# Down projection by blocks: sums one step ahead of the splits, plain tiles in the written order

## The chip, the core and the metric

The kernel runs on one core of one Trainium2 chip. The metric is device time in microseconds (us). Three runs of the kernel before gave 2416.98, 2417.23 and 2417.55 us; the median is 2417.23 us.

## The reference

The program computes two layers. Each layer has three parts, and in each the input is normalised, worked on, normalised again and added to the residual `x`. Parts one and three are feed-forward networks (SwiGLU), part two is a mixer of three branches. The change touches the feed-forward networks alone, of which there are four in a run.

```python
SEQ, D_MODEL, D_FF, DEPTH = 512, 1024, 2816, 2

def swiglu_ffn(h, w_gate, w_up, w_down):
    return (jax.nn.silu(h @ w_gate) * (h @ w_up)) @ w_down

for l in range(DEPTH):
    h = rms_norm(x, norm_pre[l, 0])
    x = x + 0.5 * rms_norm(swiglu_ffn(h, ffn1_w_gate[l], ffn1_w_up[l], ffn1_w_down[l]), norm_post[l, 0])
    ...
```

All of it is float32. The **down projection** is the last product, `hidden @ w_down`: 512 tokens by 2816 hidden values, times 2816 by 1024.

## The kernel before

**Precision.** Every operand of a matmul is split into a high part of type float32r and the rest: `hi = cast(x)` on ACT (ScalarE), `lo = x - hi` on DVE (VectorE). A product then takes three matmuls: high by high, high by low and low by high (`mm_out`, L248). So each operand costs a cast on ACT and a subtraction on DVE before PE (TensorE) can use it, and the subtraction waits for the cast.

**The hidden values** lie transposed, in 22 tiles `hid[f]` of 128 hidden values by 512 tokens. `block_tiles` (L346) makes them, and then the down projection follows.

**The down projection before** is the class `Down` (L466). Hidden tiles 2 to 17 are multiplied by blocks, with seven products in place of eight (the scheme of Strassen and Winograd): the hidden values, the tokens and the output columns are each cut into two halves, and sums and differences of blocks are multiplied. The seven products are named in `ORDER` (L470) after their left block: A11, S3, S2, A12, S1, S4, A22. Each has four **steps** c0 to c3 (`PER` is 4), and a step takes two hidden tiles: 12 matmuls of 512 columns. Tiles 0 and 1 (`MIDDLE`) and 18 to 21 (`LAST`) are multiplied plainly, 24 matmuls a tile: the two `MIDDLE` tiles after the product S1, the four `LAST` ones at the end, in `out_proj` (L253), one token tile after the other.

**What a step needs** stands in `prepare` (L497): load the weights (512 KB a quadrant; SP, the sync engine, issues all loads); where the step has a weight sum, form it on DVE (1024 columns; in products S3, S2, S1 and A22); for S2 also two sums of hidden values on DVE; then the casts `dh` and `whi` on ACT, the subtractions `dl` and `wlo` on DVE; for A12 two more sums of hidden values. In S3 a step loads two quadrants, and its sum frees them at once, since it is kept in the room of `xh`. In the other products the quadrant stays in its buffer until the step's `wlo` is done.

**What sets the order.** `run` (L573) first prepares four steps (`AHEAD`), and then, after the matmuls of step d, prepares step d+4. All that `prepare` issues on ACT and DVE is pinned: it stays in written order on its engine. `classical` (L564) makes the plain tiles: it is written after product S1, it loads, splits and multiplies at that place, and its splits go through `split` (L111), which isn't pinned, so the scheduler may place them among pinned work. `out_proj` does the same for `LAST` with the function `stat` in `ffn` (L707).

**Buffers.** `whi` and `wlo` have five each. `raw`, the loaded weights, has three tiles of two halves each; a load waits until both halves of an older tile are used up. `dh` and `dl` come from the 14 slots "s".

Of the kernel before, what the change touches and what calls it, by code (L numbers as in the profile page):

```python
# [8 lines left out]
F32 = mybir.dt.float32  # L9
F32R = mybir.dt.float32r  # L10
# [31 lines left out]
def kernel(  # L42
# [30 lines left out]
    def slot(name, dt=F32, tag="t"):  # L73
        return tp.tile([P, 512], dt, tag=tag, name=name, bufs=SLOTS[tag])

    def bank(n, tag="pb"):
        return psp.tile([P, 512], F32, tag=tag, name=n, bufs=BANKS[tag])
# [172 lines left out]
        mm(o, sh[:, t], wl, start=False, stop=False, skip_group_check=True)  # L250
        mm(o, sl[:, t], wh, start=False, stop=en, skip_group_check=True)

    def out_proj(w2d, nk, stat, tail, finish, upcoming, early, banks=None):  # L253


        ld = lambda k: load_rows(w2d, k)
        fresh = banks is None
# [208 lines left out]
    class Down:  # L466
# [5 lines left out]
        STEPS = 7 * PER  # L472
        AHEAD = 4
        MIDDLE, LAST = (0, 1), (18, 19, 20, 21)

        def __init__(self, wd, hid):
            self.wd, self.hid = wd, hid
            self.ready = {}
            self.s1 = None
            self.next = 0  # L480

        def pairs(self):

# [10 lines left out]
            else:  # L494
                pinned(nc.vector.tensor_tensor(a[:, H1], a[:, H0], a[:, H1], op=ALU.add))

        def prepare(self, d):  # L497

            if d >= self.STEPS:
                return  # L500
            j, c = divmod(d, self.PER)
            name, quads, _ = self.ORDER[j]
            f0 = self.F0 + 2 * c
            raws = []
            for half, h in quads:
                r0 = (f0 + half * self.NP) * P
                raws.append(load_raw([(lambda r: r.rearrange("p (k c) -> p k c", k=2),
                                       self.wd[r0:r0 + 2 * P, HS[h]].rearrange("(k p) c -> p k c", p=P))]))
            kept = None if j == 0 else self.kept[:, 2 * c:2 * c + 2, :].rearrange("p k c -> p (k c)")
            tt = lambda o, a, b, op: pinned(nc.vector.tensor_tensor(o, a, b, op=op))  # L510
# [12 lines left out]
            a = [self.hid[f0 + q] for q in range(2)]  # L523
            b = [self.hid[f0 + self.NP + q] for q in range(2)]
# [3 lines left out]
            part = {"A11": [x[:, H0] for x in a], "S3": [x[:, H1] for x in a], "S2": [x[:, H0] for x in a],  # L528
                    "A12": [x[:, H0] for x in b], "S4": [x[:, H0] for x in b], "A22": [x[:, H1] for x in b],
                    "S1": None}[name]  # L530
            sh, sl = (slot(x, F32R, "s").rearrange("p (k t) -> p k t", k=2) for x in ("dh", "dl"))
            hi, lo = (wp.tile([P, 1024], F32R, tag=t, name=t) for t in ("whi", "wlo"))
            if part is None:
                pinned(nc.scalar.copy(sh, self.s1[c]))
            else:
                for q in range(2):
                    pinned(nc.scalar.copy(sh[:, q], part[q]))
            pinned(nc.scalar.copy(hi, src))  # L538
            if part is None:
                tt(sl, self.s1[c], sh.bitcast(F32), ALU.subtract)  # L540
            else:
                for q in range(2):
                    tt(sl[:, q], part[q], sh[:, q].bitcast(F32), ALU.subtract)
            tt(lo, src, hi.bitcast(F32), ALU.subtract)
            if name == "A12":
                for q in range(2):
                    tt(b[q][:, H0], b[q][:, H0], a[q][:, H0], ALU.add)
            self.ready[d] = sh, sl, hi, lo

        def ahead(self):  # L550
            self.prepare(self.next)
            self.next += 1

        def product(self, d):
            j, c = divmod(d, self.PER)
            name, _, b = self.ORDER[j]
            sh, sl, hi, lo = self.ready.pop(d)
            for q in range(2):
                w = slice(q * 512, (q + 1) * 512)
                for i in range(2):  # L560
                    mm_out(self.banks[b][i], slice(i * P, (i + 1) * P), sh[:, q], sl[:, q], hi[:, w], lo[:, w],
                           st=(q == 0 and c == 0 and j in (0, 1, 3)))

        def classical(self, f, first):  # L564

            wh, wl = load_rows(self.wd, f)
            sh, sl = slot("sh", F32R, "s"), slot("sl", F32R, "s")
            split(sh, sl, self.hid[f])
            for i, h in ((2, 1), (3, 1), (2, 0), (3, 0), (0, 0), (1, 0), (0, 1), (1, 1)):
                mm_out(self.out[i][h], slice(i * P, (i + 1) * P), sh, sl, wh[:, HS[h]], wl[:, HS[h]],  # L570
                       st=(first and (i, h) in ((2, 1), (3, 1))))

        def run(self):  # L573
            a0, b0, a1, b1, c0, d0 = (bank(n) for n in ("oA", "oB", "oA", "oB", "oC", "oD"))
# [6 lines left out]
            copy = lambda o, i: pinned(nc.scalar.copy(o, i))  # L581
            while self.next < self.AHEAD:
                self.ahead()
            for d in range(self.STEPS):
                j, c = divmod(d, self.PER)
                self.product(d)
                self.ahead()
                if c < self.PER - 1:
                    continue
                if j == 0:  # L590
                    for i in range(2):
                        copy(self.p1[i], self.banks["A"][i])
                if j == 1:
                    for i in range(2):
                        copy(p7[i], self.banks["C"][i])
                if j == 2:
                    self.u2 = [slot("u2") for i in range(2)]
                    for i in range(2):
                        copy(self.u2[i], self.banks["A"][i])
                if j == 4:  # L600
                    self.u4 = [slot("u4") for i in range(2)]
                    for i in range(2):
                        copy(self.u4[i], self.banks["A"][i])
                    for i in range(2):
                        pinned(nc.vector.tensor_tensor(self.u4[i], p7[i], self.u4[i], op=ALU.subtract))
# [21 lines left out]
    def ffn(wg, wu, wd, weights, forms, arrive, finish, upcoming, early, late, begin):  # L627
# [76 lines left out]
        block_tiles(wg, wu, fs, forms, hid, between)  # L704
        late()

        def stat(f):  # L707
            sh, sl = slot("sh", F32R), slot("sl", F32R)
            split(sh, sl, hid[f])
            return sh, sl  # L710

        banks = down.run()
        return out_proj(wd, NF, stat, TAIL, lambda i, b: finish(i, down.results(i, b)), upcoming, early, banks)


    def mixer(l, wv, arrive, finish, upcoming, early):
# [585 lines left out]
```

## Time and profile before

| | us |
|---|---|
| median of three runs | 2417.23 |
| profiled execution | 2419.53 |
| its span, first to last instruction | 2417.8 |
| ACT busy | 1218.4 (50%) |
| POOL busy | 179.0 (7%) |
| time of DMA queue q1, as a share of 16 engines | 35.9% |

The profile comes from one execution. Its span is 1.7 us shorter than that run's time, and that run is 2.3 us longer than the median. For each engine the profile lists busy time; for each instruction its start, its duration, the idle time of the engine ahead of it and, where it can be told, what ended that idle time. The duration of a matmul is the time until its end is modelled; the next one starts earlier, since matmuls are pipelined. The order in which the span runs is: first layer FFN 1, mixer, FFN 2, then the second layer the same way. The four down projections begin near 244, 1081, 1444 and 2280 us.

### The profile page before, as it was taken

How to read it: one execution, taken by the hardware profiler on the slowest of the kernel's cores; microseconds unless marked ns; L12 is line 12 of the kernel's file. 1: busy time of each engine (PE TensorE's matmuls, PEld its weight loads, DVE VectorE, ACT ScalarE, POOL GpSimd, SP SyncE). 2: the span in 40 equal slices, each digit the busy share in tenths (PEclk: the TensorE clock that was granted, in tenths of full speed). 3: DMA queues.
4: the chain of work that ended last, by engine and by line, in shares of the span. 5: the costliest groups of instructions: out<-in, count | busy, mean ns of one | idle time of the engine just before them, and what ended most of it. 6: DMA issues, size and time to landing. Idle time of an engine off the chain costs nothing. (4 is left out here: it accounts for less than half of the span.)

```text
span 2417.8 us, 36165 instructions
## 1 busy us (share of the span) xinstructions
PE 2339.3 (97%) x14072; PEld 2064.9 (85%) x14072; DVE 1855.4 (77%) x2745; ACT 1218.4 (50%) x2372; POOL 179.0 (7%) x287
## 2 busy tenths in 40 slices
PE   8999989999999999998999998999999999999988
PEld 7999767887888899996799996778878888999956
DVE  7888867858965388888688888678599644888885
ACT  5556545644323355565455565466433334555552
POOL 0000001201011100000000000012010211000000
PEclk9999999999999999999999999999999999999999
DMA  5333543231333233345323345341313332333441
GB/s 167 105 105 108 205 141 97 71 92 47 112 87 105 79 87 103 104 134 192 115 83 105 105 131 190 119 115 53 109 49 107 89 105 64 98 106 104 167 161 70
DMA packets 332764, 265.33 MB, mean 110 GB/s; under 512 B 12746, under 2 KB 285164, under 8 KB 332592
## 3 DMA queue, kind: packets, MB, share of 16 engines
q1 hardware_dynamic: 332592, 263.02, 35.9%
q8 instruction: 110, 1.80, 0.3%
q14 instruction: 62, 0.51, 0.1%
HBM read 260.88 MB, written 2.10 MB: 109 GB/s over the span
## 5 line engine op out<-in xcount | busy, mean ns | idle before, releaser
L352 DVE TENSOR_TENSOR wlo<-raw,whi 128x1024 fp32r<-128x1024 f32 (+1 forms) x304 | 331.1, 1089 | 108.8 <-ACT whi L350 108.0
L113 DVE TENSOR_TENSOR wlo<-raw,whi 128x1024 fp32r<-128x1024 f32 (+1 forms) x202 | 252.4, 1257 | 200.5 <-ACT whi L112 193.7
L112 ACT CAST whi<-raw 128x1024 fp32r<-128x1024 f32 (+1 forms) x202 | 210.6, 1045 | 387.2 <-PE gate L66 131.3
L350 ACT CAST whi<-raw 128x512 fp32r<-128x512 f32 x532 | 315.4, 620 | 160.0 <-DVE raw L352 160.0
L352 DVE TENSOR_TENSOR raw<-raw 128x512 f32<-128x512 f32 x304 | 209.2, 688 | 5.8
L66 PE MATMUL A<-xh,whi 128*128 128x256 f32 x608 | 172.5, 284 | 0.0
L66 PE MATMUL A<-xh,wlo 128*128 128x256 f32 x608 | 172.0, 283 | 0.0
L66 PE MATMUL A<-xl,whi 128*128 128x256 f32 x608 | 172.0, 283 | 0.0
L892 DVE SCALAR_TENSOR_TENSOR y<-u,cw,y 128x511 f32<-128x511 f32 (+14 forms) x240 | 166.7, 756 | 0.0
L66 PE MATMUL gate<-xh,whi 128*128 128x512 f32 x384 | 151.3, 394 | 0.0
L66 PE MATMUL gate<-xh,wlo 128*128 128x512 f32 x384 | 149.8, 390 | 1.3 <-DVE wlo L113 1.3
L66 PE MATMUL gate<-xl,whi 128*128 128x512 f32 x384 | 149.6, 390 | 0.0
L200 POOL TENSOR_TENSOR rs<-ms,mhalf 128x1 f32<-128x1 f32 x48 | 28.2, 588 | 1513.1 <-DVE ms L198 1513.1
L510 DVE TENSOR_TENSOR wlo<-raw,whi 128x1024 fp32r<-128x1024 f32 x80 | 97.8, 1222 | 50.1 <-ACT whi L538 50.1
L538 ACT CAST whi<-raw 128x1024 fp32r<-128x1024 f32 x80 | 84.1, 1051 | 93.3 <-PE oA L66 38.1
L66 PE MATMUL oA<-wlo,dh 128*128 128x512 f32 x256 | 103.5, 404 | 18.5 <-DVE wlo L510 18.5
L350 ACT COPY cp<-A 128x256 f32<-128x256 f32 x228 | 84.5, 370 | 70.6 <-PE A L66 69.7
L66 PEld LDWEIGHTS A<-xl,whi 128*128 128x128 f32 x608 | 116.6, 192 | 0.2
L66 PEld LDWEIGHTS A<-xh,whi 128*128 128x128 f32 x608 | 116.5, 192 | 0.2
L66 PEld LDWEIGHTS A<-xh,wlo 128*128 128x128 f32 x608 | 116.6, 192 | 0.0
L66 PE MATMUL oA<-whi,dh 128*128 128x512 f32 x256 | 101.3, 396 | 4.8 <-ACT whi L538 4.8
L66 PE MATMUL oA<-whi,dl 128*128 128x512 f32 x256 | 100.0, 390 | 0.0
(346 smaller groups left out, 7183.8 us busy)
## 6 DMA issues: line engine op xcount, KB each, us to landing
raw<-in_ffn_w_down_dram SPq DMA_DIRECT2D x152, 512.0 KB, 4.6
raw<-in_w_in_dram SPq DMA_DIRECT2D x108, 512.0 KB, 4.7
raw<-in_ffn_w_gate_dram SPq DMA_DIRECT2D x152, 256.0 KB, 3.4
raw<-in_ffn_w_up_dram SPq DMA_DIRECT2D x152, 256.0 KB, 4.6
raw<-in_w_branch_dram SPq DMA_DIRECT2D x24, 512.0 KB, 3.7
raw<-in_w_out_dram SPq DMA_DIRECT2D x16, 512.0 KB, 4.2
raw<-in_ffn_w_gate_dram SPq DMA_DIRECT2D x12, 512.0 KB, 5.1
raw<-in_ffn_w_up_dram SPq DMA_DIRECT2D x12, 512.0 KB, 4.6
```

The costliest lines, as they stand in the source:

```text
L66: tc.keep_in_program_order(nc.tensor.matmul(*a, **k))
L112: nc.scalar.copy(hi, src)
L113: nc.vector.tensor_tensor(lo, src, hi.bitcast(F32), op=ALU.subtract)
L200: nc.gpsimd.tensor_tensor(rs, ms, mhalf[:, 0:1], op=ALU.pow)
L350: copy = lambda o, i: pin(nc.scalar.copy(o, i))
L352: tt = lambda o, a, b, op: pin(nc.vector.tensor_tensor(o, a, b, op=op))
L510: tt = lambda o, a, b, op: pinned(nc.vector.tensor_tensor(o, a, b, op=op))
L538: pinned(nc.scalar.copy(hi, src))
L892: nc.vector.scalar_tensor_tensor(y[:, back:], u[:, :S - back], cw[:, c, j:j + 1], y[:, back:], op0=ALU.mult, op1=ALU.add)
```

## The change

`prepare` is divided in two. `sums(p)` issues the loads of step p and then what it adds up on DVE: the weight sum, and for S2 first the two sums of hidden values and then the weight sum. `parts(p)` issues the casts and the two kinds of subtraction. `ahead` calls `sums(p + 1)` and then `parts(p)`, so on DVE the sums of a step stand in front of the subtractions of the step before it.

The plain tiles become steps as well. `plan` writes one list: five products (A11 to S1), `MIDDLE`, the products S4 and A22, `LAST`. `classical` and `stat` are gone; a plain tile is loaded by `sums`, split by `parts` and multiplied by `product`, four steps behind its preparation. `out_proj` gets the four `LAST` tiles ready-made (`head`). The splits of the plain tiles are thereby pinned, their slots are those of `dh` and `dl`, and the cast and subtraction of S1 and of plain tiles go over 512 columns at once. The matmuls and their order on PE stay as they were, and so does the number of instructions of each kind on ACT and DVE.

```diff
-    def out_proj(w2d, nk, stat, tail, finish, upcoming, early, banks=None):
+    def out_proj(w2d, nk, stat, tail, finish, upcoming, early, head=None):
...
+        else:
+            banks, rest = head
...
-        rest = [(k, ld(k), stat(k)) for k in range(nk - tail, nk)]
+        if fresh:
+            rest = [(k, ld(k), stat(k)) for k in range(nk - tail, nk)]
...
+        def plan(self):
+
+            self.steps = [(j, c) for j in range(5) for c in range(self.PER)]
+            self.steps += [(None, f) for f in self.MIDDLE]
+            self.steps += [(j, c) for j in (5, 6) for c in range(self.PER)]
+            self.end = len(self.steps)
+            self.steps += [(None, f) for f in self.LAST]
...
+        def sums(self, p):
+
+            self.load(p)
+            j, c = self.steps[p]
+            if j is None:
+                return
+            name, raws = self.ORDER[j][0], self.raw[p]
...
             if name == "S2":
+                for q, x in enumerate(self.of(p)):
+                    tt(x, self.s1[c][:, q], x, ALU.add)
                 tt(kept, kept, raws[0], ALU.subtract)
                 src = kept
...
-            if name == "S2":
-                for q in range(2):
-                    tt(a[q][:, H0], self.s1[c][:, q], a[q][:, H0], ALU.add)
...
+        def parts(self, p):
+
+            j, c = self.steps[p]
+            sh, sl = (slot(x, F32R, "s") for x in ("dh", "dl"))
             hi, lo = (wp.tile([P, 1024], F32R, tag=t, name=t) for t in ("whi", "wlo"))
...
+            of, src = self.of(p), self.raw.pop(p)
+            n = 512 // len(of)
+            cut = [slice(q * n, (q + 1) * n) for q in range(len(of))]
+            for q, x in zip(cut, of):
+                pinned(nc.scalar.copy(sh[:, q], x))
             pinned(nc.scalar.copy(hi, src))
...
+            for q, x in zip(cut, of):
+                pinned(nc.vector.tensor_tensor(sl[:, q], x, sh[:, q].bitcast(F32), op=ALU.subtract))
+            pinned(nc.vector.tensor_tensor(lo, src, hi.bitcast(F32), op=ALU.subtract))
...
         def ahead(self):
-            self.prepare(self.next)
+
+            p = self.next
+            if p == 0:
+                self.sums(0)
+            if p + 1 < len(self.steps):
+                self.sums(p + 1)
+            if p < len(self.steps):
+                self.parts(p)
             self.next += 1
...
-        def classical(self, f, first):
-
-            wh, wl = load_rows(self.wd, f)
-            sh, sl = slot("sh", F32R, "s"), slot("sl", F32R, "s")
-            split(sh, sl, self.hid[f])
...
             while self.next < self.AHEAD:
                 self.ahead()
-            for d in range(self.STEPS):
-                j, c = divmod(d, self.PER)
-                self.product(d)
+            for p in range(self.end):
+                j, c = self.steps[p]
+                self.product(p)
                 self.ahead()
...
-                    for f in self.MIDDLE:
-                        self.classical(f, f == self.MIDDLE[0])
-            return self.out
+            while self.next < len(self.steps):
+                self.ahead()
+            rest = []
+            for p in range(self.end, len(self.steps)):
+                sh, sl, hi, lo = self.ready[p]
+                rest.append((self.steps[p][1], (hi, lo), (sh, sl)))
+            return self.out, rest
```

Three places show it. The first is DVE where product S2 begins, in the first down projection. `xh` is the kept weight sum, `hid<-S` the two sums of hidden values, `dl` and `wlo` the low parts. Before, from the low part of step S3 c3 through step S2 c1:

```order
L510 TENSOR_TENSOR wlo<-xh,whi 128x1024
L510 TENSOR_TENSOR xh<-xh,raw 128x1024
L510 TENSOR_TENSOR hid<-S_648,hid 128x256 x2
L510 TENSOR_TENSOR dl<-hid,dh 128x256 x2
L510 TENSOR_TENSOR wlo<-xh,whi 128x1024
L510 TENSOR_TENSOR xh<-xh,raw 128x1024
L510 TENSOR_TENSOR hid<-S_649,hid 128x256 x2
L510 TENSOR_TENSOR dl<-hid,dh 128x256 x2
L510 TENSOR_TENSOR wlo<-xh,whi 128x1024
```

Now, from the sums of step S2 c0 to the low parts of the same step:

```order
L540 TENSOR_TENSOR hid<-S_648,hid 128x256 x2
L540 TENSOR_TENSOR xh<-xh,raw 128x1024
L569 TENSOR_TENSOR dl<-hid,dh 128x256 x2
L570 TENSOR_TENSOR wlo<-xh,whi 128x1024
L540 TENSOR_TENSOR hid<-S_649,hid 128x256 x2
L540 TENSOR_TENSOR xh<-xh,raw 128x1024
L569 TENSOR_TENSOR dl<-hid,dh 128x256 x2
L570 TENSOR_TENSOR wlo<-xh,whi 128x1024
```

The sums of a step have moved past the low parts of the step before: between a sum and the low part made from it there now stand the other step's `dl` and `wlo` and the next step's sums.

The second place is DVE where the down projection begins. Before, from the low parts of step A11 c3 (`wlo<-raw`) to the second weight difference of S3:

```order
L510 TENSOR_TENSOR dl<-hid,dh 128x256 x2
L510 TENSOR_TENSOR wlo<-raw,whi 128x1024
L510 TENSOR_TENSOR xh<-raw 128x1024
L510 TENSOR_TENSOR dl<-hid,dh 128x256 x2
L510 TENSOR_TENSOR wlo<-xh,whi 128x1024
L510 TENSOR_TENSOR xh<-raw 128x1024
```

Now, from the first weight difference of S3 (step c0) to the third:

```order
L540 TENSOR_TENSOR xh<-raw 128x1024
L569 TENSOR_TENSOR dl<-hid,dh 128x256 x2
L570 TENSOR_TENSOR wlo<-raw,whi 128x1024
L540 TENSOR_TENSOR xh<-raw 128x1024
L569 TENSOR_TENSOR dl<-hid,dh 128x256 x2
L570 TENSOR_TENSOR wlo<-xh,whi 128x1024
L540 TENSOR_TENSOR xh<-raw 128x1024
```

Each weight difference, and with it the need for its loaded quadrants, has moved ahead by one pair of low parts.

The third place is ACT around the `MIDDLE` tiles. `u` is a copy of a PSUM bank that frees it for the plain tiles; `sh` (before) and `dh<-hid 128x512` (now) are the high parts of plain hidden tiles. Before, from the last step of S4 that is prepared ahead:

```order
L537 CAST dh<-hid 128x256 x2
L538 CAST whi<-raw 128x1024
L581 COPY u_3559<-oA 128x512
L581 COPY u_3560<-oA 128x512
L112 CAST whi<-raw 128x1024
L112 CAST sh<-hid 128x512 x4
L537 CAST dh<-hid 128x256 x2
L112 CAST sh<-hid 128x512
L112 CAST whi<-raw 128x1024
L538 CAST whi<-raw 128x1024
```

Now, from the first `MIDDLE` tile through the copies:

```order
L566 CAST dh<-hid 128x512
L567 CAST whi<-raw 128x1024
L566 CAST dh<-hid 128x512
L567 CAST whi<-raw 128x1024
L566 CAST dh<-hid 128x256 x2
L567 CAST whi<-raw 128x1024
L566 CAST dh<-hid 128x256 x2
L567 CAST whi<-raw 128x1024
L613 COPY u_3557<-oA 128x512
L613 COPY u_3558<-oA 128x512
```

Both `MIDDLE` tiles have moved ahead of all four steps of S4, of which two now stand ahead of the copies, and the cast of the second tile's weights has moved up to that of the first.

More of the change, by code (lines that the diff above doesn't have):

```diff
@@ L251, in mm_out @@
         mm(o, sl[:, t], wh, start=False, stop=en, skip_group_check=True)
-    def out_proj(w2d, nk, stat, tail, finish, upcoming, early, banks=None):
+    def out_proj(w2d, nk, stat, tail, finish, upcoming, early, head=None):
         ld = lambda k: load_rows(w2d, k)
-        fresh = banks is None
+        fresh = head is None
         if fresh:
             banks = [[bank(f"o{i}{h}", "pb" if i < 3 else "pa") for h in range(2)] for i in range(NT)]
+        else:
+            banks, rest = head
         def mms(i, h, k, sh, sl, wh, wl):
@@ L471 @@
                  ("A12", ((1, 0),), "B"), ("S1", ((1, 1),), "A"), ("S4", ((1, 1),), "A"), ("A22", ((1, 0),), "C"))
-        STEPS = 7 * PER
         AHEAD = 4
@@ L480, in __init__ @@
             self.next = 0
+            self.raw = {}
+            self.plan()
         def pairs(self):
@@ L495, in sum_tokens, with of, load @@
                 pinned(nc.vector.tensor_tensor(a[:, H1], a[:, H0], a[:, H1], op=ALU.add))
-        def prepare(self, d):
-            if d >= self.STEPS:
+        def plan(self):
[4 more added lines that the diff above has]
+            self.steps += [(None, f) for f in self.LAST]
+        def of(self, p):
+            j, c = self.steps[p]
+            if j is None:
+                return [self.hid[c]]
+            f0 = self.F0 + 2 * c
+            a, b = ([self.hid[f0 + n + q] for q in range(2)] for n in (0, self.NP))
+            return {"A11": lambda: [x[:, H0] for x in a], "S3": lambda: [x[:, H1] for x in a],
+                    "S2": lambda: [x[:, H0] for x in a], "A12": lambda: [x[:, H0] for x in b],
+                    "S4": lambda: [x[:, H0] for x in b], "A22": lambda: [x[:, H1] for x in b],
+                    "S1": lambda: [self.s1[c].rearrange("p k t -> p (k t)")]}[self.ORDER[j][0]]()
+        def load(self, p):
+            j, c = self.steps[p]
+            if j is None:
+                self.raw[p] = load_raw([(lambda r: r, self.wd[c * P:(c + 1) * P, :])])
                 return
-            j, c = divmod(d, self.PER)
-            name, quads, _ = self.ORDER[j]
-            f0 = self.F0 + 2 * c
             raws = []
-            for half, h in quads:
-                r0 = (f0 + half * self.NP) * P
+            for half, h in self.ORDER[j][1]:
+                r0 = (self.F0 + 2 * c + half * self.NP) * P
                 raws.append(load_raw([(lambda r: r.rearrange("p (k c) -> p k c", k=2),
                                        self.wd[r0:r0 + 2 * P, HS[h]].rearrange("(k p) c -> p k c", p=P))]))
+            self.raw[p] = raws
+        def sums(self, p):
+            self.load(p)
+            j, c = self.steps[p]
+            if j is None:
+                return
+            name, raws = self.ORDER[j][0], self.raw[p]
+            tt = lambda o, a, b, op: pinned(nc.vector.tensor_tensor(o, a, b, op=op))
             kept = None if j == 0 else self.kept[:, 2 * c:2 * c + 2, :].rearrange("p k c -> p (k c)")
-            tt = lambda o, a, b, op: pinned(nc.vector.tensor_tensor(o, a, b, op=op))
             src = raws[0]
@@ L544, in prepare @@
[L544 to L548, printed above, removed]
-        def ahead(self):
-            self.prepare(self.next)
-            self.next += 1
[L554 to L557, printed above, removed]
+            self.raw[p] = src
@@ new lines, in parts @@
+        def parts(self, p):
+            j, c = self.steps[p]
+            sh, sl = (slot(x, F32R, "s") for x in ("dh", "dl"))
+            hi, lo = (wp.tile([P, 1024], F32R, tag=t, name=t) for t in ("whi", "wlo"))
+            of, src = self.of(p), self.raw.pop(p)
[3 more added lines that the diff above has]
+                pinned(nc.scalar.copy(sh[:, q], x))
+            pinned(nc.scalar.copy(hi, src))
+            for q, x in zip(cut, of):
+                pinned(nc.vector.tensor_tensor(sl[:, q], x, sh[:, q].bitcast(F32), op=ALU.subtract))
+            pinned(nc.vector.tensor_tensor(lo, src, hi.bitcast(F32), op=ALU.subtract))
+            if j is not None and self.ORDER[j][0] == "A12":
+                for q, x in enumerate(of):
+                    pinned(nc.vector.tensor_tensor(x, x, self.hid[self.F0 + 2 * c + q][:, H0], op=ALU.add))
+            self.ready[p] = sh, sl, hi, lo
@@ new lines, in ahead, with product @@
+        def ahead(self):
+            p = self.next
[5 more added lines that the diff above has]
+                self.parts(p)
+            self.next += 1
+        def product(self, p):
+            j, c = self.steps[p]
+            sh, sl, hi, lo = self.ready.pop(p)
+            if j is None:
+                for i, h in ((2, 1), (3, 1), (2, 0), (3, 0), (0, 0), (1, 0), (0, 1), (1, 1)):
+                    mm_out(self.out[i][h], slice(i * P, (i + 1) * P), sh, sl, hi[:, HS[h]], lo[:, HS[h]],
+                           st=(c == self.MIDDLE[0] and (i, h) in ((2, 1), (3, 1))))
+                return
+            b = self.banks[self.ORDER[j][2]]
@@ L560, in product @@
                 for i in range(2):
-                    mm_out(self.banks[b][i], slice(i * P, (i + 1) * P), sh[:, q], sl[:, q], hi[:, w], lo[:, w],
-                           st=(q == 0 and c == 0 and j in (0, 1, 3)))
-        def classical(self, f, first):
-            wh, wl = load_rows(self.wd, f)
-            sh, sl = slot("sh", F32R, "s"), slot("sl", F32R, "s")
-            split(sh, sl, self.hid[f])
-            for i, h in ((2, 1), (3, 1), (2, 0), (3, 0), (0, 0), (1, 0), (0, 1), (1, 1)):
-                mm_out(self.out[i][h], slice(i * P, (i + 1) * P), sh, sl, wh[:, HS[h]], wl[:, HS[h]],
-                       st=(first and (i, h) in ((2, 1), (3, 1))))
+                    t = slice(q * 256 + i * P, q * 256 + (i + 1) * P)
+                    mm_out(b[i], t, sh, sl, hi[:, w], lo[:, w], st=(q == 0 and c == 0 and j in (0, 1, 3)))
         def run(self):
@@ L580, in run, with tap @@
             p7 = [taps[:, 2 + i, :] for i in range(2)]
-            copy = lambda o, i: pinned(nc.scalar.copy(o, i))
+            def tap(o, b):
+                for i in range(2):
+                    pinned(nc.scalar.copy(o[i], self.banks[b][i]))
             while self.next < self.AHEAD:
                 self.ahead()
-            for d in range(self.STEPS):
-                j, c = divmod(d, self.PER)
-                self.product(d)
+            for p in range(self.end):
+                j, c = self.steps[p]
+                self.product(p)
                 self.ahead()
-                if c < self.PER - 1:
+                if c != self.PER - 1:
                     continue
                 if j == 0:
-                    for i in range(2):
-                        copy(self.p1[i], self.banks["A"][i])
+                    tap(self.p1, "A")
                 if j == 1:
-                    for i in range(2):
-                        copy(p7[i], self.banks["C"][i])
+                    tap(p7, "C")
                 if j == 2:
                     self.u2 = [slot("u2") for i in range(2)]
-                    for i in range(2):
-                        copy(self.u2[i], self.banks["A"][i])
+                    tap(self.u2, "A")
                 if j == 4:
                     self.u4 = [slot("u4") for i in range(2)]
-                    for i in range(2):
-                        copy(self.u4[i], self.banks["A"][i])
+                    tap(self.u4, "A")
                     for i in range(2):
                         pinned(nc.vector.tensor_tensor(self.u4[i], p7[i], self.u4[i], op=ALU.subtract))
-                    for f in self.MIDDLE:
-                        self.classical(f, f == self.MIDDLE[0])
-            return self.out
+            while self.next < len(self.steps):
[5 more added lines that the diff above has]
+            return self.out, rest
         def results(self, i, banks):
@@ L705, in ffn @@
         late()
[L707 to L713, printed above, removed]
+        head = down.run()
+        return out_proj(wd, NF, None, TAIL, lambda i, b: finish(i, down.results(i, b)), upcoming, early, head)
     def mixer(l, wv, arrive, finish, upcoming, early):
```

16 lines of the change are left out of this document (removed).

## Prediction

> **What bounds the kernel now.** First the page's head: who is busy all the time.
>
> ```profile
> span 2417.8 us, 36165 instructions
> PE 2339.3 (97%) x14072; PEld 2064.9 (85%) x14072; DVE 1855.4 (77%) x2745; ACT 1218.4 (50%) x2372; POOL 179.0 (7%) x287
> ```
>
> PE sets the time; the change leaves its matmuls alone, so only what PE loses to waits can be won. Next the view of waits, PE's own: who it waited for, total, times, longest.
>
> ```profile
> PE oA L66 <- DVE wlo L510: 18.5, 32, 0.8
> PE oD L66 <- ACT sh L112: 18.5, 4, 4.6
> PE oD L66 <- DVE wlo L113: 8.5, 8, 1.4
> ...
> PE oA L66 <- ACT whi L538: 4.8, 12, 0.4
> PE oD L66 <- ACT whi L112: 4.5, 4, 1.1
> ```
>
> All five belong to the four down projections (`oA` to `oD` are their banks) and sum to 54.8 us, 13.7 in each. The stretches of the first one tell where: S3, S2, S1, plain tiles (the columns: length, then PE busy).
>
> ```profile
> 244.30:263.00 18.70, 18.70 (x85) 15.48 (x85) 16.52 (x24) 9.56 (x18) 0.00 (x0) 1.00 0.93 317
> 263.00:280.60 17.60, 13.77 (x54) 9.46 (x53) 14.92 (x26) 8.46 (x17) 0.00 (x0) 1.00 0.41 140
> ...
> 293.50:308.30 14.80, 12.66 (x50) 8.70 (x49) 12.58 (x16) 8.40 (x15) 0.00 (x0) 1.00 0.38 131
> 308.30:329.40 21.10, 13.24 (x38) 9.52 (x39) 12.73 (x19) 8.38 (x15) 0.00 (x0) 0.76 0.50 176
> ```
>
> Idle: none, 3.83 in S2, 2.14 in S1, 7.86 at the plain tiles.
>
> But idle time isn't all that is lost, for a matmul counts as busy beyond the start of the next. The timeline of PE gives the true pitch (start, duration, idle before).
>
> ```profile
> 244.36 0.40 PE L66 MATMUL oA<-whi,dh 128*128 128x512 f32 x1
> ...
> 266.15 0.39 PE L66 MATMUL oA<-whi,dh 128*128 128x512 f32 x1
> 266.86 0.50 PE L66 MATMUL oA<-wlo,dh 128*128 128x512 f32 x1 [0.32 <-DVE wlo L510]
> ```
>
> Eight steps of 12 matmuls without a wait take 266.15 - 244.36 = 21.79: 0.227 a matmul, 2.72 a step. The last down projection, 480 matmuls with nothing between them, starts and ends at
>
> ```profile
> 2280.20 0.40 PE L66 MATMUL oA<-whi,dh 128*128 128x512 f32 x1
> ...
> 2410.18 0.39 PE L66 MATMUL oD<-whi,sl 128*128 128x512 f32 x1
> ```
>
> that is 129.98, where 479 x 0.227 = 108.7 would do. So 21.2 us are lost in each, **85.0 in the four** (the counts of the waits divide by four): 55 idle, the rest refilling after each wait and half-speed matmuls after the long ones:
>
> ```profile
> 307.88 0.39 PE L66 MATMUL oA<-whi,dl 128*128 128x512 f32 x1
> 312.89 0.79 PE L66 MATMUL oD<-whi,sh 128*128 128x512 f32 x1 [4.62 <-ACT sh L112]
> ...
> 316.67 0.63 PE L66 MATMUL oD<-wlo,sh 128*128 128x512 f32 x1
> 317.10 0.63 PE L66 MATMUL oD<-whi,sl 128*128 128x512 f32 x1
> ...
> 312.30:319.12 6.83, 4.87 (x10) 3.37 (x11) 6.83 (x11) 3.34 (x8) 0.00 (x0) 0.50 0.62 223
> ...
> 325.95:329.36 3.41, 3.41 (x9) 2.63 (x8) 0.00 (x0) 0.00 (x0) 0.00 (x0) 0.50 0.82 301
> ```
>
> The pitch is 0.43 there, and the granted clock in the last two rows 0.50.
>
> **The plain tiles.** ACT and DVE at that place:
>
> ```profile
> 311.27 1.05 ACT L112 CAST whi<-raw 128x1024 fp32r<-128x1024 f32 x1
> 312.22 2.18 ACT L112 CAST sh<-hid 128x512 fp32r<-128x512 f32 x4
> ...
> 322.58 1.04 ACT L112 CAST whi<-raw 128x1024 fp32r<-128x1024 f32 x1 [3.66 <-PE oA L66]
> ...
> 310.76 0.75 DVE L510 TENSOR_TENSOR dl<-hid,dh 128x256 fp32r<-128x256 f32 x2
> 311.43 1.22 DVE L510 TENSOR_TENSOR wlo<-raw,whi 128x1024 fp32r<-128x1024 f32 x1
> 312.57 1.29 DVE L605 TENSOR_TENSOR u<-xl,u 128x512 f32<-128x512 f32 x2
> 313.77 1.22 DVE L113 TENSOR_TENSOR wlo<-raw,whi 128x1024 fp32r<-128x1024 f32 x1
> ```
>
> PE has been done with S1 at 308.1, but the first tile's casts stand behind all of S4's and the copies, and the second tile's cast waits for the first tile's matmuls to free a buffer. Now both tiles are prepared ahead of S4, four steps before PE wants them, as S4 and A22 are. From these starts DVE's pitch is 0.67 for two `dl`, 1.14 for a 1024-column operation, 0.60 for a 512-column one. A plain step costs DVE 0.60 + 1.14 = 1.74 and gives PE 24 matmuls, 5.45; an S4 step 1.81 against 2.72. So DVE gains lead here: I take the whole loss as gone. A22 (1.14 + 1.81 = 2.95) loses 0.23 a step, 0.9 in all, against at least one step of lead.
>
> What the copies now wait behind: two S4 steps on ACT, prepared ahead anyway, while PE still works on the last S1 step; the bank that they free (`oA`) is the last that a plain tile writes, after 18 matmuls or 4.1 us. I cost this at nothing. If that cover fails, the two copies (1.05) and two steps of ACT (1.6 each: 0.55, a quarter of the 2.18, and 1.05) show: up to 4 us a projection.
>
> **S2.** DVE's timeline before:
>
> ```profile
> 258.71 1.22 DVE L510 TENSOR_TENSOR xh<-raw 128x1024 f32<-128x1024 f32 x1
> ...
> 262.26 1.22 DVE L510 TENSOR_TENSOR xh<-xh,raw 128x1024 f32<-128x1024 f32 x1
> ...
> 265.58 1.22 DVE L510 TENSOR_TENSOR wlo<-xh,whi 128x1024 fp32r<-128x1024 f32 x1 [0.53 <-ACT whi L538]
> ...
> 270.03 1.23 DVE L510 TENSOR_TENSOR wlo<-xh,whi 128x1024 fp32r<-128x1024 f32 x1 [0.52 <-ACT whi L538]
> ```
>
> An S2 step takes DVE 270.03 - 265.58 = 4.45; its work is 1.14 + 0.67 + 0.67 + 1.14 = 3.62, the rest waits for the casts, which wait for the sum just made. With the sum a step ahead the casts run beside the other step's low parts, and 3.62 remains. That is still above PE's 2.72: **S2 stays bound by DVE**, and what PE loses is how late DVE arrives.
>
> Follow DVE to the low part of S2 c0. An S3 step took 3.55 (258.71 to 262.26), its work is 2.95; the last weight difference of S3, at 258.71 before, gains 0.60 three times, and 1.81 since it now stands ahead of a pair of low parts: 255.1. Here a new wait can come in, for the quadrants. They are issued as
>
> ```profile
> 249.30 0.88 SPq L124 DMA_DIRECT2D raw<-in_ffn_w_down_dram  x2
> ...
> DMA to landing us min/median/max: 7.1/7.5/8.0
> ...
> DMA to landing us min/median/max: 5.5/5.8/6.1
> ```
>
> (the last row: the same place of the last down projection) and with 7.1 and 8.0 us to landing they are there at 256.4 and 257.7, before 258.71 but 2.6 after 255.1. Behind the waiting difference on DVE stand the low parts of S3 and all of S2, for which PE waits. The issue stays near 249.3, for the buffer is still freed by A11's last `wlo`; the loads in front move up a little. The delay lies between 0 (no DVE operation of this stage shows a wait for a landing now) and 2.6; nearest to these rows I take 2.3: 257.4. From there to the end of `wlo` of S2 c0: 1.14 (S3's sum), 1.81 (low parts), 1.81 (S2's first sums), 1.81, 1.81, 0.67 and 1.22: 267.7. PE wants it at 266.15 + 0.23 = 266.4, waits 1.3, and then 0.9 in each of the next two steps; the fourth follows after 1.81, in time. So 3.1 us remain, plus 0.1 of refill (266.86 was followed 0.33 later by the next matmul) for three waits: **3.4**. In the last down projection landings are 1.6 to 1.9 shorter (5.5/5.8/6.1), and I take 1.6 off: 1.8.
>
> **S1.** DVE's step is 1.14 + 0.60 + 1.14 = 2.88 without the cast's wait, 0.16 over PE's. From PE's last wait in S2 to the first S1 operand PE has six steps, 16.3; DVE has 1.81 + 4 x 1.81 + 4 x 0.67 + 2 x 1.14 + 1.74 = 15.75. The lead of 0.6 shrinks by 0.16 twice and then grows: no wait, by a margin of 0.25.
>
> **Sum.** Lost now 85.0; left 3 x 3.4 + 1.8 = 12.0; saved 73.0. Against its own execution, 2419.5 (span 2417.8) becomes 2346.5; the median is 2.3 lower: **2344**.
>
> [...] In the rows above the clock is at 0.50 after the wait of 4.62, but also for 3.41 us after waits of 1.13 and 0.77 alone (the idle time at the second tile). [...]
>
> **Rivals.**
>
> - *The quadrants land in time.* For it: the loads in front are issued earlier, no DVE wait for a landing shows now. Then `wlo` of S2 c0 ends at 265.4, and only about 0.8 and some refill are lost, 1.0 a projection: 81 saved, 2336. Against it: 257.7 against 255.1.
> - *Half speed remains in S2.* One stretch of 3.41 at 0.50 in each costs 1.7, in all 6.8: 2351. Against it: S2 now has seven waits of up to 0.76 and the clock in its row is 1.00.
> - *S1 keeps its waits* (the margin is 0.25): 2.14 idle and about 0.9 of refill in each: 12, so 2356.
> - *The plain tiles keep theirs*, because their buffers or banks still come late, by the 4 us above in each: 16, so 2360.
> - *Slower than before.* DVE runs in written order, so a sum whose quadrant hasn't landed holds up finished work behind it. If that happens at all 16 summed steps, the step's pitch becomes that of a load. It decides from 2.72 + 21.2 / 16 = 4.05 us a step; at 4.6, the median to landing in the page's list of issues, 16 x 0.55 = 8.8 a projection are added: 2452.
>
> ```profile
> raw<-in_ffn_w_down_dram SPq DMA_DIRECT2D x152, 512.0 KB, 4.6
> ```
>
>   Against it: outside S3 a step needs one quadrant, not two, and no landing shows as a wait now. [...]
> - *It doesn't do what it says*, and the scheduler keeps the old order: 2417. The order of the instructions speaks against it.
>
> **How the numbers follow.** Forecast 2344: 0.52. Landing in time: 0.20. Half speed: 0.10. S1: 0.07. Plain tiles: 0.06. Slower: 0.02. No effect: 0.02. The rest, 0.01, is lost elsewhere and slightly faster. The range takes in the first three whole, with the bounds of the landing (2336 and, at 2.6 with half speed on top, 2352), and most of the next: 2334 to 2359. A measurement tells apart about 0.2% (5 us). Faster by more than that: 0.96; within: 0.02; slower: 0.02.
>
> **What would show it.** Right: the waits on `sh` and the 4.62 are gone, as is every granted clock of 0.50 in the down projections; PE waits only for `wlo` in S2, two or three times, 1.3 at most; DVE waits for a landing at S3's third or fourth weight difference; its S2 pitch is 3.6. Wrong: waits on `oD`, waits in S1, or DVE idle at sums of S2, S1 or A22. The step that I trust least is the 2.3 of the landing.

## The result and the profile after

The changed kernel takes 2345.02 us (median of 4 runs, 2344.26 to 2345.22), the kernel before beside it 2417.39 (4 runs, 2416.98 to 2419.08). The ratio is 0.9699, with a 95% interval from 0.9682 to 0.9716. The forecast was 2344, in a range from 2334 to 2359. The profiled execution took 2344.83.

First the head of the page of the kernel after.

```profile
span 2343.1 us, 36173 instructions
PE 2311.7 (99%) x14072; PEld 2057.4 (88%) x14072; DVE 1849.1 (79%) x2745; ACT 1219.6 (52%) x2372; POOL 183.1 (8%) x287
```

No engine has less to do: DVE and ACT are busy for as long as before (1849 against 1855, 1220 against 1218). The span is 74.7 shorter, and PE's busy time 27.6. For the same 14072 matmuls that means that fewer of them ran long.

PE's waits in the kernel after, as before: who it waited for, total, times, longest. The first row is the longest wait left in the program, and it isn't in a down projection.

```profile
PE pt L71 <- DVE hn L215: 7.7, 1, 7.7
PE oA L66 <- DVE wlo L570: 6.8, 12, 0.6
...
PE oC L66 <- DVE wlo L570: 0.9, 2, 0.6
```

Of the 54.8 us of the five rows before, 7.7 are left, in 14 waits of at most 0.6, all for `wlo`. The waits on `oD`, which were the plain tiles', are gone. The same stretches of the first down projection in the kernel after, S2, the end of A12, S1, and the plain tiles (length, PE, PEld, DVE, ACT, POOL busy, granted clock, DMA share, GB/s):

```profile
263.00:276.80 13.80, 12.03 (x51) 8.92 (x50) 13.80 (x25) 8.81 (x17) 0.00 (x0) 1.00 0.49 172
280.60:289.00 8.40, 8.40 (x39) 6.96 (x38) 8.40 (x15) 3.59 (x6) 0.00 (x0) 1.00 0.55 180
289.00:304.00 15.00, 15.00 (x68) 12.43 (x67) 15.00 (x19) 12.68 (x22) 0.00 (x0) 1.00 0.60 221
304.00:316.00 12.00, 12.00 (x55) 9.94 (x54) 10.69 (x16) 4.48 (x9) 0.00 (x0) 1.00 0.60 211
```

PE idles for 1.77 us in S2 (3.83 before) and not at all from there on. In S2 DVE is busy for all of the 13.80: there it is the bound. At the plain tiles the clock, 0.76 in the row before, is 1.00.

How long each down projection takes, from the start of PE's first matmul into `oA` to the start of its last into `oD`, comes from PE's timeline. For the last one, in the kernel after:

```profile
2223.94 0.40 PE L66 MATMUL oA<-whi,dh 128*128 128x512 f32 x1
...
2335.47 0.39 PE L66 MATMUL oD<-whi,dl 128*128 128x512 f32 x1
```

2335.47 - 2223.94 = 111.53. Read in the same way (the last line is an experiment below, in which the view of waits has no row of a down projection left):

| us | FFN 1 | FFN 2 | FFN 3 | FFN 4 | sum |
|---|---|---|---|---|---|
| before | 131.70 | 131.28 | 130.69 | 129.98 | 523.65 |
| after | 112.19 | 113.71 | 111.84 | 111.53 | 449.27 |
| e7_pool_late | 109.85 | 110.45 | 110.26 | 109.61 | 440.17 |

The four projections are shorter by 74.4, which is all of the 74.7 but 0.3. So next to nothing was won or lost elsewhere.

What holds up S2 begins earlier, where DVE prepares S3 and waits for loaded quadrants. DVE's timeline of the kernel after, from the third weight difference of S3 to the second low part of S2 (start, duration, idle before and what ended it):

```profile
253.60 1.23 DVE L540 TENSOR_TENSOR xh<-raw 128x1024 f32<-128x1024 f32 x1 [1.67 <-DMA raw<-in_ffn_w_down_dram]
...
256.55 1.22 DVE L540 TENSOR_TENSOR xh<-raw 128x1024 f32<-128x1024 f32 x1
...
265.57 1.23 DVE L570 TENSOR_TENSOR wlo<-xh,whi 128x1024 fp32r<-128x1024 f32 x1
...
269.18 1.23 DVE L570 TENSOR_TENSOR wlo<-xh,whi 128x1024 fp32r<-128x1024 f32 x1
```

and on PE, from the same kernel:

```profile
266.85 0.50 PE L66 MATMUL oA<-wlo,dh 128*128 128x512 f32 x1 [0.57 <-DVE wlo L570]
...
270.46 0.50 PE L66 MATMUL oA<-wlo,dh 128*128 128x512 f32 x1 [0.60 <-DVE wlo L570]
```

and DVE's waits for loaded quadrants in the whole run:

```profile
DVE xh L540 <- DMA raw<-in_ffn_w_down_dram: 8.0, 5, 2.1
```

DVE's step in S2 is 3.61 (269.18 - 265.57), and PE, which needs 2.72, waits once in each of three steps (the third wait is at 274.08, 0.60 again). The low part ends right where PE goes on (265.57 + 1.23 = 266.80, and PE starts at 266.85).

### The profile page after: what moved, and what is told of

It is laid out like the page before. It is cut to its first block, busy times and chain, and to the rows that moved or that the text cites. A ratio compares the mean times of both kernels' runs of the same rounds, so it can differ in the third digit from the quotient of the medians.

```text
span 2343.1 us, 36173 instructions
## 1 busy us (share of the span) xinstructions
PE 2311.7 (99%) x14072; PEld 2057.4 (88%) x14072; DVE 1849.1 (79%) x2745; ACT 1219.6 (52%) x2372; POOL 183.1 (8%) x287
## 5 line engine op out<-in xcount | busy, mean ns | idle before, releaser
L355 DVE TENSOR_TENSOR wlo<-raw,whi 128x1024 fp32r<-128x1024 f32 (+1 forms) x304 | 331.3, 1090 | 108.7 <-ACT whi L353 107.9
L112 ACT CAST whi<-raw 128x1024 fp32r<-128x1024 f32 (+2 forms) x178 | 185.2, 1043 | 353.8 <-PE gate L66 131.4
L113 DVE TENSOR_TENSOR wlo<-raw,whi 128x1024 fp32r<-128x1024 f32 (+2 forms) x178 | 223.3, 1264 | 168.6 <-ACT whi L112 161.7
L567 ACT CAST whi<-raw 128x1024 fp32r<-128x1024 f32 x104 | 109.4, 1052 | 85.3 <-issue 36.1
L570 DVE TENSOR_TENSOR wlo<-raw,whi 128x1024 fp32r<-128x1024 f32 x104 | 128.4, 1235 | 24.8 <-ACT whi L567 24.8
L66 PE MATMUL oA<-wlo,dh 128*128 128x512 f32 x304 | 119.8, 394 | 6.8 <-DVE wlo L570 6.8
L66 PE MATMUL oA<-whi,dh 128*128 128x512 f32 x304 | 118.4, 389 | 0.0
L66 PE MATMUL oA<-whi,dl 128*128 128x512 f32 x304 | 118.4, 389 | 0.0
```

Of the source, the lines that this page charges most:

```text
L66: tc.keep_in_program_order(nc.tensor.matmul(*a, **k))
L113: nc.vector.tensor_tensor(lo, src, hi.bitcast(F32), op=ALU.subtract)
L355: tt = lambda o, a, b, op: pin(nc.vector.tensor_tensor(o, a, b, op=op))
L570: pinned(nc.vector.tensor_tensor(lo, src, hi.bitcast(F32), op=ALU.subtract))
```

## The experiments

There were three questions: do the two parts of the change bring what the forecast gave to each; is what is left the wait for quadrants and DVE's S2 step; and does it go when these are taken away? The first three kernels ran on one chip, beside a median of 2418.54 for the kernel before, the other four on another, beside 2417.32.

**e1_plain_only: the plain tiles in written order, the sums where they were.** The changed kernel, with the sums of a step put back in front of its own parts, and S2's sums in their old order.

```diff
             if name == "S2":
+                tt(kept, kept, raws[0], ALU.subtract)
                 for q, x in enumerate(self.of(p)):
                     tt(x, self.s1[c][:, q], x, ALU.add)
-                tt(kept, kept, raws[0], ALU.subtract)
...
             p = self.next
-            if p == 0:
-                self.sums(0)
-            if p + 1 < len(self.steps):
-                self.sums(p + 1)
             if p < len(self.steps):
+                self.sums(p)
                 self.parts(p)
```

> The plain tiles as steps, but the sums of a step stand again at its own splits, as before the change. Theory (two independent losses: the plain tiles lose PE about 12.3 us a projection, S2 and S1 together about 8.9, that is 3.83 + 2.14 idle and 0.26 for each of 11 waits): the waits on sh and every clock of 0.50 in the projections are gone, the waits on wlo in S2 and S1 are back; against the changed kernel (2.8 left a projection) 4 x 6.1 = 24 more, 2369 us. Rival (the plain tiles are late because DVE is late with its sums): the wait of 4.62 stays, and the time is near 2400.

Measured: 2369.14 (2367.94 to 2370.23), ratio 0.9794 (0.9778 to 0.981). PE's waits in it:

```profile
PE oA L66 <- DVE wlo L570: 18.9, 32, 0.8
...
PE oA L66 <- ACT whi L567: 4.8, 13, 0.4
```

These are the two rows on `oA` of before (18.5 in 32, 4.8 in 12); the rows on `oD` are gone, and the granted clock is 1.00 in all four projections. So the plain tiles alone bring 49.4, and they keep no wait.

**e2_sums_only: the sums one step ahead, the plain tiles as they were.** The kernel before, with `prepare` divided.

```diff
-        def prepare(self, d):
+        def sums(self, d):
...
+            self.held[d] = src
+
+        def prepare(self, d):
...
+            src = self.held.pop(d)
...
         def ahead(self):
+            if self.next == 0:
+                self.sums(0)
+            self.sums(self.next + 1)
             self.prepare(self.next)
```

> The sums one step ahead, but the plain tiles loaded, split and multiplied at their own place as before the change. Theory: S2 and S1 lose as little as in the changed kernel, the plain tiles all of their 12.3 us a projection, with the clock at 0.50 twice in each: 2345 + 4 x 12.3 = 2394 us; e1's and e2's gains on 2417 add up to that of the change, 48 + 23 = 71 of 72. Rival (one cause for both): the plain tiles' wait shrinks with the sums, and the time is 2345 to 2360.

Measured: 2394.36 (2392.57 to 2394.68), ratio 0.9898 (0.9884 to 0.9913). PE's waits in it:

```profile
PE oD L66 <- DVE wlo L113: 16.4, 8, 3.4
PE oD L66 <- ACT sh L112: 10.9, 4, 2.8
...
PE oA L66 <- DVE wlo L535: 6.8, 12, 0.6
PE oD L66 <- ACT whi L112: 4.5, 4, 1.1
```

The waits on `oA` are those of the kernel after, to the tenth; the rows on `oD` come to 31.8 in place of 31.5. Between those rows the wait has moved: in the four projections PE waits 7.6 less for `sh` and 7.9 more for the plain tiles' `wlo`. In sum the plain tiles' wait doesn't shrink with the sums, which speaks against the rival. The clock is still granted at half at the plain tiles. At the second one of the first projection, in e2:

```profile
315.57:318.98 3.41, 1.52 (x6) 0.87 (x6) 1.22 (x1) 1.04 (x1) 0.00 (x0) 1.00 0.00 0
318.98:322.40 3.42, 3.42 (x10) 2.65 (x9) 0.00 (x0) 0.00 (x0) 0.00 (x0) 0.50 0.00 0
```

24.2 for the sums and 49.4 for the plain tiles make 73.6, and both together brought 72.4: the parts add up, within the scatter of the medians.

**e3_s1_late: S1's sums back beside their own step.** The changed kernel, where only S2 and A22 keep their lead.

```diff
+            late = lambda s: s < len(self.steps) and self.steps[s][0] == 4
             if p == 0:
                 self.sums(0)
-            if p + 1 < len(self.steps):
+            if late(p):
+                self.sums(p)
+            if p + 1 < len(self.steps) and not late(p + 1):
                 self.sums(p + 1)
```

> The changed kernel, with the weight sums of product S1 alone back at their own splits. Theory (the forecast's narrow lead in S1, some 0.6 us when S1 begins): DVE's S1 step is 3.6 instead of 2.9 with the cast's wait in it, against PE's 2.72, so PE waits again for wlo in S1's later steps, about 1.4 us a projection: 2350.5 us. Rival (DVE's lead in S1 is ample, the gain of S1 came from S2's): no wait in S1, 2345 us.

Measured: 2351.89 (2350.97 to 2352.26), ratio 0.9724 (0.9709 to 0.9738); against the kernel before on either chip that is 0.0025 more than the change as it is, 6 us. PE's waits in it:

```profile
PE oA L66 <- DVE wlo L570: 11.1, 20, 0.6
```

12 waits have become 20, two in S1 of each projection. The low parts on DVE show why. In e3, in S1:

```profile
292.25 1.23 DVE L570 TENSOR_TENSOR wlo<-raw,whi 128x1024 fp32r<-128x1024 f32 x1 [0.93 <-ACT whi L567]
...
295.86 1.23 DVE L570 TENSOR_TENSOR wlo<-raw,whi 128x1024 fp32r<-128x1024 f32 x1 [0.65 <-ACT whi L567]
```

and in the kernel after:

```profile
288.51 1.24 DVE L570 TENSOR_TENSOR wlo<-raw,whi 128x1024 fp32r<-128x1024 f32 x1
...
291.38 1.24 DVE L570 TENSOR_TENSOR wlo<-raw,whi 128x1024 fp32r<-128x1024 f32 x1
```

A step of 3.61 with the wait for the cast, and 2.87 without it: the gap that the sum one step ahead fills.

**e4_same_again** is the changed kernel once more, as the measure for the next three.

> The changed kernel once more, on the chip of the next three, as their measure: 2345 us by every theory.

Measured: 2345.60 (2343.89 to 2346.07), ratio 0.9701 (0.9687 to 0.9714).

**e5_late_norms: the loads of the norm rows moved behind the quadrants.** In the kernel after, two loads of norm rows (`g`) stand on SP's queue among those of the down projection. They are moved behind product S2, and the quadrants' loads are pinned, so that this order holds.

```diff
                 if j == 2:
+                    late()
                     self.u2 = [slot("u2") for i in range(2)]
...
         block_tiles(wg, wu, fs, forms, hid, between)
-        late()
 
-        head = down.run()
+        head = down.run(late)
```

> The changed kernel with the two norm rows (512 KB each) loaded after product S2 instead of among the quadrants of S3. Theory (DVE's waits for S3's third weight difference, 1.67, 2.12 and 0.99, 1.33, 1.91 us in the four projections, are a queue of loads with the norm rows in it): the quadrants land some 1.3 us earlier, the waits fall to 0 to 0.7, and PE's wait in S2 falls with them, by 1.3 to 2.5 a projection: 2338 us, 2337 to 2341. Rival (the quadrants wait for their buffer, not for the rows): the waits stay within 0.4 us, and the time is 2345 to 2346.

Measured: 2342.06 (2341.1 to 2343.19), ratio 0.9688 (0.9674 to 0.9701): 3.5 less than e4, not 8, and outside the theory's range. DVE's waits for quadrants, in e4:

```profile
DVE xh L540 <- DMA raw<-in_ffn_w_down_dram: 7.9, 5, 1.9
```

and in e5:

```profile
DVE xh L544 <- DMA raw<-in_ffn_w_down_dram: 5.4, 5, 2.1
```

PE's waits for `wlo` in the down projections fall with them, from 7.7 in 14 to 5.8 in 10. So the norm rows, with the order that the edit pins, are a part of DVE's wait, but the smaller one. SP's timeline of the kernel after, in the first and in the last projection, shows where they stand (start, length of the row's stretch, instruction, count):

```profile
246.08 0.35 SPq L185 DMA_DIRECT2D g<-in_norm_pre_dram  x1
...
2217.20 0.34 SPq L185 DMA_DIRECT2D g<-in_norm_post_dram  x1
2217.58 21.20 SPq L124 DMA_DIRECT2D raw<-in_ffn_w_down_dram  x13
```

In the first one a norm row is issued 7.5 us ahead of the end of DVE's wait (253.60). There the wait shrinks, in e5, from 1.67 to

```profile
252.26 1.22 DVE L544 TENSOR_TENSOR xh<-raw 128x1024 f32<-128x1024 f32 x1 [0.99 <-DMA raw<-in_ffn_w_down_dram]
...
2230.67 1.23 DVE L544 TENSOR_TENSOR xh<-raw 128x1024 f32<-128x1024 f32 x1 [2.10 <-DMA raw<-in_ffn_w_down_dram]
```

0.99. In the last one the only norm row is issued 16 us ahead of the end of the wait, thirteen loads follow it without another, and the wait stays: 1.91 in the kernel after, 2.10 here. So most of the delay is the quadrants' own: when their buffers come free, and how long they take to land. The trace of the kernel after shows both. In the last projection S3's first difference, the last reader of two quadrants, and the loads behind it are at

```profile
2225.83 1.22 DVE L540 TENSOR_TENSOR xh<-raw 128x1024 f32<-128x1024 f32 x1
...
2227.07 11.71 SPq L124 DMA_DIRECT2D raw<-in_ffn_w_down_dram  x10
```

The difference ends at 2227.05 and the loads start 0.02 later; in the other three projections that gap is 0.03. So SP holds nothing back: it waits for the buffer. The wait of S3's third difference ends when the second of these loads, issued at 2227.49, has landed: 6.1 later, at 2233.61. DVE would have wanted the quadrants at 2233.71 - 1.91 = 2231.80, 4.75 after the buffer came free. An earlier buffer (a fourth tile `raw`) or a shorter landing should each shorten the wait; no run here tries either, and why a landing takes 6 us stays open.

**e6_pool_adds: S2's sums of hidden values on POOL.** One line of the changed kernel.

```diff
                 for q, x in enumerate(self.of(p)):
-                    tt(x, self.s1[c][:, q], x, ALU.add)
+                    pinned(nc.gpsimd.tensor_tensor(x, self.s1[c][:, q], x, op=ALU.add))
```

> The changed kernel with S2's two sums of hidden values on POOL, which is idle there, instead of DVE. Theory (what is left in S2 is DVE's work alone): DVE's S2 step falls from 3.61 to 2.95 us, by the first S2 operand it is 1.3 earlier, and PE waits in one projection at most, about 1 us: 2336 us. Rival (POOL and DVE slow each other, or POOL's two adds, 0.65 to 0.8 each by half of its 512-column ones, come too late for the casts): no gain or a loss, 2345 or more.

Measured: 2338.71 (2337.66 to 2339.68), ratio 0.9673 (0.966 to 0.9687): 6.9 less than e4. Of PE's waits for `wlo` in the down projections these are left:

```profile
PE oC L66 <- DVE wlo L570: 2.1, 2, 1.1
```

The 12 on `oA` are gone, because DVE's S2 step no longer holds the adds. The first two low parts of S2 in e6, and the matmuls on PE that take them:

```profile
264.57 1.22 DVE L570 TENSOR_TENSOR wlo<-xh,whi 128x1024 fp32r<-128x1024 f32 x1
...
267.51 1.22 DVE L570 TENSOR_TENSOR wlo<-xh,whi 128x1024 fp32r<-128x1024 f32 x1
...
265.85 0.50 PE L66 MATMUL oA<-wlo,dh 128*128 128x512 f32 x1
...
268.79 0.50 PE L66 MATMUL oA<-wlo,dh 128*128 128x512 f32 x1
```

DVE's step is 2.94 in place of 3.61, and PE's is 2.94 too (268.79 - 265.85). So S2 was bound by DVE's step, as the forecast had it, and it still is: 2.94 against the 2.72 that PE needs. No wait shows this, for the 0.2 a step hide in the time by which a matmul counts as busy beyond the start of the next: in S2 of the second projection of e6 one at 1082.52 counts as busy for 0.39 us, and the next starts 0.32 later, where 0.23 is the pitch without waits. The second half of the theory missed. The first low part of S2 wasn't 1.3 earlier: counted from PE's first matmul of the projection it comes after 21.16 us in e6 (264.57 - 243.41) and after 21.45 in e4 (264.49 - 243.04). And PE waits in two projections, not one, for low parts of S3; the last section shows what made those late.

**e7_pool_late: both edits together.**

> Both of the two before: the adds on POOL and the norm rows after S2. Theory: no wait of PE is left in the down projections, 2334 to 2335 us, little under the adds on POOL alone, since these already leave almost no wait for the earlier loads to take away. Rival (each removes its own loss): the two gains add up, 2329 us.

Measured: 2335.86 (2335.17 to 2336.32, 5 runs), ratio 0.9662 (0.9649 to 0.9675). No wait of PE for `wlo` in a down projection is left, and DVE waits for a quadrant twice:

```profile
DVE xh L544 <- DMA raw<-in_ffn_w_down_dram: 1.0, 2, 0.5
```

This is the best version measured, 9.7 us under e4 on the same chip. The time is 0.9 above the theory's range, but the gains of e5 and e6 (3.5 and 6.9) nearly add up, as the rival had it; its 2329 was too low because it added the larger gains that were forecast for the two. What is left is small: in S2 PE still keeps to DVE's pace, 2.94 a step, where a step without waits takes 2.72.

## Why the prediction held, step by step

**The plain tiles: the whole loss gone.** Right. No wait on `oD` is left, in the kernel after or in e1, and the bank that the copies free comes in time; PE goes through the plain tiles without idling. The clock goes with them: it is at half at the plain tiles of e2 and at 1.00 in the rows of the kernel after. The share of the plain tiles, 49.4, is two thirds of the gain.

**S2: bound by DVE, a step of 3.62.** Right: 3.61, and e6 shows that the step itself is the bound. The first low part ended 0.9 earlier than worked out, at 266.80 and not 267.7, since the wait in S3 was shorter.

**The landing.** The mechanism was right, the size and the place were not. It was put at S3's last difference, with 2.3 us and a start at 257.4; in the first projection it came one difference earlier, with 1.67, and the last began at 256.55. In the second there were two waits, and in the last the wait was no shorter than in the first. DVE's timeline of the kernel after, in these two:

```profile
1071.36 1.23 DVE L540 TENSOR_TENSOR xh<-raw 128x1024 f32<-128x1024 f32 x1 [2.12 <-DMA raw<-in_ffn_w_down_dram]
...
1075.37 1.23 DVE L540 TENSOR_TENSOR xh<-raw 128x1024 f32<-128x1024 f32 x1 [0.99 <-DMA raw<-in_ffn_w_down_dram]
...
2233.71 1.23 DVE L540 TENSOR_TENSOR xh<-raw 128x1024 f32<-128x1024 f32 x1 [1.91 <-DMA raw<-in_ffn_w_down_dram]
```

Two steps of the forecast failed here. It followed the loads of S3's last difference alone. In the first projection these go out at 249.02, near the 249.3 that it had, and have landed at 256.28, just before DVE wants them at 256.55. The loads of the third difference had no term in the sum, though the signs name it beside the fourth. They go out at 247.21, when S3's first difference has freed their buffer, DVE wants them at 251.93 (253.60 - 1.67), and the second of them lands at 253.57. And the forecast took 1.6 off in the last projection, because landings were shorter there before. Now the second load of the third difference takes 6.0, 6.3, 5.5 and 6.1 us from issue to landing in the four projections, so there was nothing to take off: times to landing read from the trace of before were carried over to a kernel in which the loads and the need for them stand elsewhere.

**S1: no wait, by a margin of 0.25.** Right in all four projections, and e3 shows what that lead is worth: 6, not the 12 of its rival. The rival was priced at all that S1 lost before, when S2's sums were late too. With S1's sums alone late, only its last two steps on PE are longer than 2.72 (3.4 to 3.6), with a wait of about 0.6 each; in e1, where S2's sums are late as well, all four are (3.3 to 3.9).

**The sum.** 73.0 were to be saved, the projections show 74.4. The yardstick of 0.227 a matmul holds: in e7 every product but S3 and S2 takes 10.9 on PE for its 48 matmuls. What it leaves out is 0.9 in each of the first three projections, before and after, where PE does eight transposes for the next part (`pt`, L71) among the `LAST` tiles; the last projection, from which 21.2 was read, has none. With these, four projections without a loss take 4 x 108.7 + 3 x 0.9 = 437.5. So 523.65 - 437.5 = 86.2 were lost before, 1.2 more than the forecast's 85.0, for the last projection lost less than the others on average; and 449.27 - 437.5 = 11.8 are left, against 12.0. That the second number is so close is partly luck: by projection 2.6, 4.1, 2.2 and 2.8 are left, where the forecast had 3.4 three times and 1.8, and the errors of the landing cancel in the sum. The 2.3 us by which the profiled execution lay above the median before was taken off, but the one after lies 0.2 below its median; so 2344 came out 1.0 low, though 1.7 more was saved between the two profiles than forecast.

**The rivals.** The first, quadrants that land in time, didn't come about: DVE waits for them in all four. A DVE that holds up finished work at every sum didn't come about: five waits at 64 sums. Half speed in S2 didn't either (1.00 in its row above), and e1 is the sharper test, for there S2 has waits of 0.76 in a row. A stretch of one S2 step in e1:

```profile
268.00:271.40 3.40, 2.24 (x9) 1.30 (x9) 2.74 (x6) 1.69 (x3) 0.00 (x0) 1.00 0.61 217
```

PE is busy in 2.24 of 3.40 us, and the clock stays at 1.00. The stretch of before, ahead of the second one at half speed:

```profile
322.54:325.95 3.41, 1.51 (x6) 1.04 (x6) 1.23 (x1) 1.04 (x1) 0.00 (x0) 1.00 0.08 6
```

1.51 of 3.41, and then 3.41 us at 0.50; the row of e2 above, with 1.52, was followed by 0.50 as well. Another stretch of e2, where S1 ends and the wait for the plain tiles begins in the last projection, stayed at 1.00 and was followed by 3.4 us more at 1.00:

```profile
2315.78:2319.19 3.41, 1.69 (x8) 1.08 (x6) 3.41 (x6) 3.12 (x7) 0.00 (x0) 1.00 0.86 279
```

So in this kernel the clock also went down without one long wait: the longest in that stretch of before is 1.13 us. In the traces of before and after, cut into stretches of 3.41 us from the first change of the granted clock on, PE is busy for 0.00 to 1.51 us in each of the eight stretches at 1.00 that go ahead of one at 0.50, and for at least 2.2 in all the others at 1.00. Of the two rows of e2, 1.52 was followed by 0.50 and 1.69 by 1.00.

## What to carry to other kernels

Where an engine works in written order and a result must go to a second engine and come back, the wait is filled by writing the next step's independent work between the two (DVE's step in S1: 3.61 us with the wait for the cast, 2.87 without), and the price to look for is a load that this work now needs sooner (here 8.0 us of DVE's waits). Unscheduled pieces that stand at one place among scheduled ones cost more than the pieces: here two plain tiles brought two thirds of the gain, because they could only start once the work in front of them was over. For the sum, look at what else the engine does in the stretch that the yardstick is laid on, and don't take one stretch for all. And read the pitch beside the waits: an engine can keep to another's pace without a wait in the view (PE in S2 of e6: 2.94 us a step, as DVE).

## What the runs showed of the hardware beyond that

**Adds moved to POOL freed no time on DVE as a whole.** e6 takes 32 adds off DVE, 12.1 us in e4. The heads of the pages of e4,

```profile
PE 2310.7 (99%) x14072; PEld 2056.3 (88%) x14072; DVE 1849.0 (79%) x2745; ACT 1220.5 (52%) x2372; POOL 179.0 (8%) x287
```

and of e6:

```profile
PE 2311.2 (99%) x14072; PEld 2056.1 (88%) x14072; DVE 1851.3 (79%) x2713; ACT 1218.4 (52%) x2372; POOL 220.9 (9%) x319
```

DVE has 32 instructions less and is busy for 2.3 us more. The groups of instructions, by shape, say where (busy, mean ns of one). In e4, the longest group of low parts, and the adds:

```profile
L570 DVE TENSOR_TENSOR wlo<-raw,whi 128x1024 fp32r<-128x1024 f32 x104 | 126.8, 1219 | 24.9 <-ACT whi L567 24.9
...
L540 DVE TENSOR_TENSOR hid<-S,hid 128x256 f32<-128x256 f32 x32 | 12.1, 419 | 0.0
```

In e6, the low parts:

```profile
L570 DVE TENSOR_TENSOR wlo<-raw,whi 128x1024 fp32r<-128x1024 f32 x104 | 133.6, 1284 | 20.9 <-ACT whi L567 20.9
```

and the adds on POOL:

```profile
L548 POOL TENSOR_TENSOR hid<-S,hid 128x256 f32<-128x256 f32 x32 | 41.9, 1334 | 866.1 <-DVE dl L569 866.1
```

An add takes 1.33 us on POOL (0.85 to 2.0) and 0.42 on DVE, and while POOL adds, DVE's subtractions take longer. One beside an add, a low part of A11 in the first projection of e6:

```profile
240.10 1.76 DVE L570 TENSOR_TENSOR wlo<-raw,whi 128x1024 fp32r<-128x1024 f32 x1
```

1.76 in place of 1.22. DVE's busy time without the adds grew by 12.1 + 2.3 = 14.4, which is 0.45 an add: about what an add took on DVE itself. What e6 gains is the place: the adds run mostly beside A11's low parts, for which PE doesn't wait, and no longer in S2, where DVE is the bound. It isn't free there: the last adds also fall beside S3's second difference (1.75 in place of 1.22), so that S3's low parts come later. Over the four projections PE's S2 is 7.9 shorter than in e4 and its S3 2.5 longer.
